# A decoder block on one Trainium2 core: the mixer's output projection as seven block products

## The chip, the cores and the metric

One core of one Trainium2 chip runs the whole kernel, with its five engines: TensorE (PE) for matmuls and transposes, VectorE (DVE), ScalarE (ACT), GpSimd (POOL), and SyncE (SP), which here only issues DMAs. The metric is the device time of one execution in microseconds. Inputs and output are float32 in HBM.

## The reference

One decoder block on 1024 tokens of width 1024. A normed input feeds two branches, a state-space one (S5) and a forgetting attention (FoX). Each is gated, their sum goes through one output projection, and a memory attention and a gated FFN follow:

```python
h = x
u = rms_norm(h, norm_mix)
proj = u @ w_in
...
out_a = glu_a * jax.nn.sigmoid(glu_b)              # glu_a, glu_b = split(gelu(s5) @ w_glu)
out_b = att @ w_fox_o
h = h + (gate_a * out_a + gate_b * out_b) @ w_mix_out
h = h + memory_cross_attention(rms_norm(h, norm_mem_q), rms_norm(mem, norm_mem_kv), w_mem_q, w_mem_kv, w_mem_o)
f_a, f_b = split(rms_norm(h, norm_ffn) @ w_ffn_in)
h = h + (silu(f_a) * f_b) @ w_ffn_out
out = rms_norm(h, norm_final)
```

The line with `w_mix_out`, a product of 1024x1024 by 1024x1024, is the mixer's projection, and the one that is edited.

## The kernel before

**Products.** TensorE works on fp32r operands, which keep fewer bits than fp32. So an operand is split into a high part, a cast on ACT (L183, the helper `split`), and a low part, the rest, by a subtraction on VectorE or GpSimd (L184; GpSimd where `pool_lo` is set). A product is three matmuls, hi·hi, hi·lo and lo·hi, added up in a PSUM bank (`mm3`, L173 to L175). A bank holds 128x512 values. There are eight: three "mm", two "sc", two "pv" and one "misc".

**Order.** The program is written stage by stage, but a scheduler decides the order of each engine's instructions, by priority and by when it expects the operands. Each engine then works through its list in order, and an instruction that waits holds up all behind it. Tiles come from pools with a fixed number of buffers: an allocation waits until the oldest buffer has been read for the last time. `weave(main, side, lead)` mixes two lists of steps in the text; `behind(...)` holds steps back until a named instruction is placed. Nearly all DMAs are issued by SP, in one queue: one that waits holds up the rest.

**The stage of the change** is the first half of `stage_tail`. Activations lie transposed: channels on partitions, tokens along the free axis.

- For each of 8 channel blocks j of 128, `glu.values` and `glu.rest` make the gated unit: products, a copy (L1239), a sigmoid on ACT (L1244), a product on VectorE (L1245) and the gate on GpSimd (L1252) with `ga`, loaded by SP. The result is a tile `sg` of 128x1024.
- `fox_part(j)` (L604) multiplies the attention's output by `w_fox_o` (fox weights, two j at a time), takes the product times the gate half `gb` (L616), adds it to `sg` (L617) and splits the sum into `mT`, the mixer's left operand. It runs three j behind the gated unit.
- `mix_weights` fetches and splits `w_mix_out`. `mix(t, c)` (L664) makes the 128x512 output tile of token tile t and column half c: 8 channel blocks by 3 matmuls, 24, and one VectorE add of the bank to a half-row of x, into H[t] (L668). There are 16 such tiles.
- `ahead(j)` prepares the FFN's weights for j = 0 to 2 (adds and splits on VectorE and ACT, kept in DRAM as `w_d`). Its steps are woven into the first twelve mixer tiles.
- `norm(t)` normalises H[t]: squares on ACT (L190), four small VectorE operations and one GpSimd power (L207 to L217, the power at L211), the scaling of a 128x1024 tile `xs` on VectorE (L231; one buffer), eight transposes in two banks (L237), and splits of the turned blocks into `u2`. Norms 0 to 3 lie behind the last four mixer tiles; norms 4 to 7 are woven with the memory queries `mem_q(h, 0)`, whose weights `wq` are four 128x1024 blocks, split whole.

Of the kernel before, what the change touches and what calls it, by code (L numbers as in the profile page):

```python
# [9 lines left out]
F32 = mybir.dt.float32  # L10
F32R = mybir.dt.float32r
# [3 lines left out]
ALU = mybir.AluOpType  # L15
# [4 lines left out]
P = 128  # L20
D = 1024
L = 1024
NT = 8
# [8 lines left out]
RAW = 1072  # L32

WSLOT = 1088
# [84 lines left out]
class Block:  # L119
# [126 lines left out]
    def norm_turn(self, xs, act, t):  # L246

        for b in range(2):
            cast = self.turned(self.turn(xs, b, ("misc", "pv")[b]), b, act, t)
        return cast  # L250

    def warm(self, n):
# [329 lines left out]
def stage_tail(B, big, s2, sh, x, glu, aT, gate_d, kv_d, w_fox_o, w_mix_out, g_mq, w_mem_q, w_mem_o, g_ffn,  # L582
               w_ffn_in, w_ffn_out, g_fin, out):
    nc, V, A, G, T, S, small, ident = B.nc, B.V, B.A, B.G, B.T, B.S, B.small, B.ident
    NS2 = 16

    def bslot(dt=F32, name="b"):
        return big.tile([P, D], dt, tag="big", name=name)

    def slot(dt=F32, name="t"):  # L590
        return s2.tile([P, D], dt, tag="t", bufs=NS2, name=name)
# [3 lines left out]
    def load(src, name):  # L595
        t_ = sh.half(name)
        S.dma_start(t_, src)
        return t_


    mT = Act(s2, "t", NS2, 8, L, name="mx")
    fox = {}

    def fox_part(j):  # L604
        if j % 2 == 0:
            with B.behind(glu.after):
                fox[j // 2] = B.wblock(w_fox_o, 0, 4, j * P, 2 * P)
        fh, fl = fox[j // 2]
        o = (j % 2) * P
        sg = glu.out.pop(j)  # L610
        for h in range(2):
            cs = slice(512 * h, 512 * h + 512)
            po = B.bank(("pv", "pv", "misc")[(2 * j + h) % 3])
            B.gemm_t(po, fh[:, :, o:o + P], fl[:, :, o:o + P], aT, h, 4)
            gb = load(gate_d[D + j * P:D + (j + 1) * P, cs], "gb")
            V.tensor_mul(gb, gb, po)  # L616
            V.tensor_add(sg[:, cs], sg[:, cs], gb)  # L617
            mh, ml = mT.rhs(j, h)
            merged.append(B.split(mh, ml, sg[:, cs]))

    merged = []
# [8 lines left out]
    for j in range(5, 8):  # L630
        fox_part(j)


    H = [bslot(name=f"h{t}") for t in range(NT)]
    gq = B.bcast_gain(s2, g_mq)
    u2 = Act(s2, "t", NS2, 8, L, name="u2")
# [6 lines left out]
    def wslots(src, pool_lo):  # L643

        nk = src.shape[0] // P
        raw = B.wpool.tile([P, RAW], F32, tag="raw", bufs=4, name="raw")[:, :D]
        S.dma_start(raw.rearrange("p (k c) -> p k c", k=nk), src.rearrange("(k p) c -> p k c", p=P))
        hl = bslot(F32R, "wbh"), bslot(F32R, "wbl")
        B.split(*hl, raw, pool_lo)
        return [t_.rearrange("p (k c) -> p k c", k=nk) for t_ in hl]  # L650

    def mix_weights(c):

        wm = ([], [])
        for kk in range(4):
            if c == 0:
                hl = B.wblock(w_mix_out, 2 * kk, 2, 0, 512)
            else:
                hl = wslots(w_mix_out[2 * kk * P:(2 * kk + 2) * P, 512:D], False)
            for w_, t_ in zip(wm, hl):  # L660
                w_ += [t_[:, 0, :], t_[:, 1, :]]
        return wm

    def mix(t, c, wm):  # L664
        cs = slice(512 * c, 512 * c + 512)
        ps = B.bank()
        gemm_n(ps, mT, t, wm, 8)
        V.tensor_add(H[t][:, cs], ps, load(x[t * P:(t + 1) * P, cs], "xr"))  # L668

    def norm(t, gb, act):  # L670
        xs = s2.tile([P, D], F32, tag="xs", bufs=1, name="xs")
        B.norm_scale(xs, H[t], B.rstd(H[t]), gb)
        return B.norm_turn(xs, act, t)


    AHEAD_IN = 2
# [1 line left out]
    pre = {}  # L678

    def ahead(j):  # L680
# [52 lines left out]

        return [fetch, plain, sums, seventh, rest] if j < AHEAD_IN else [first, plain]

    wm0 = mix_weights(0)
    with B.behind(merged[-1]):
        wm1 = mix_weights(1)
    mixes = [lambda t=t: mix(t, 0, wm0) for t in range(NT)] + [lambda t=t: mix(t, 1, wm1) for t in range(4)]
# [268 lines left out]
    gs = {}  # L1008

    def gated(p):  # L1010
        ge, go = gs.pop(2 * p), gs.pop(2 * p + 1)
# [979 lines left out]
```

## Time and profile before

| what | value |
|---|---|
| median of 3 runs | 1540.18 us (1540.08 to 1541.64) |
| span of the profiled execution | 1538.1 us |
| that execution's own time beside its span | not recorded; the median of the runs is 2.1 us above the span |
| TensorE busy | 1520.7 us (99%) |
| VectorE busy | 1005.7 us (65%) |
| ScalarE busy | 658.1 us (43%) |
| GpSimd busy | 253.6 us (16%) |
| first and last add of the mixer's tiles to H | 692.6 and 769.8 us |

Times in the trace count from the start of the span. A line of a view names the kernel's line, the engine, the operation, the tiles (written<-read), the shape and how often. In a group "| busy, mean ns of one | idle before <-releaser" follow: the busy sum, the mean duration, and how long the engine stood idle just before, with what ended that. In a timeline a row starts with its start and its duration, and square brackets hold the idle time before it. Matmuls overlap, so a matmul's own duration is longer than its distance to the next.

### The profile page before, as it was taken

What the parts mean: (1) busy time and instruction counts of PE and PEld (TensorE: products, weight loads), DVE (VectorE), ACT (ScalarE), POOL (GpSimd) and SP (SyncE); (2) the same over time, 40 slices, a digit from 0 to 9 for tenths busy, and PEclk for the clock granted to TensorE, in tenths of its full rate; (3) what the DMA queues carried; (4) which work ended last, traced back from release to release, by engine and by line L of the source; (5) the groups of instructions that cost most, each with busy time, mean ns of one, the idle gap of its engine ahead of it and who ended that gap; (6) DMA issues with size and microseconds to landing.
All of it is one profiled execution on the core that took longest, in us unless ns stands there. A gap on an engine that the chain in (4) does not pass through costs nothing. (4 is left out here: it accounts for less than half of the span.)

```text
span 1538.1 us, 20434 instructions
## 1 busy us (share of the span) xinstructions
PE 1520.7 (99%) x7329; PEld 1257.7 (82%) x7329; DVE 1005.7 (65%) x1828; ACT 658.1 (43%) x1183; POOL 253.6 (16%) x341
## 2 busy tenths in 40 slices
PE   8999999999999999999999999999999999999998
PEld 7888888898777678888888888888888888888886
DVE  7936554355878867675556797777777775675555
ACT  7423334324667643232435663333333333354343
POOL 1166542100121214100102200000000000101001
PEclk9999999999999999999999999999999999999999
DMA  9634556611223746378210356555544544896542
GB/s 286 161 104 102 131 128 144 180 41 16 50 46 88 192 131 198 111 218 308 89 69 1 117 204 210 162 161 160 158 158 157 157 145 139 291 391 220 192 163 110
DMA packets 196293, 234.06 MB, mean 152 GB/s; under 512 B 35576, under 2 KB 127656, under 8 KB 195680
## 3 DMA queue, kind: packets, MB, share of 16 engines
q1 hardware_dynamic: 188704, 214.93, 47.0%
q10 hardware_dynamic: 7488, 17.83, 3.1%
q8 instruction: 57, 0.93, 0.3%
q14 instruction: 44, 0.36, 0.1%
HBM read 161.94 MB, written 72.71 MB: 153 GB/s over the span
## 5 line engine op out<-in xcount | busy, mean ns | idle before, releaser
L184 DVE TENSOR_TENSOR wlo<-raw,whi 128x1024 fp32r<-128x1024 f32 (+2 forms) x120 | 126.3, 1058 | 45.4 <-ACT whi L183 44.2
L183 ACT CAST whi<-raw 128x1024 fp32r<-128x1024 f32 (+2 forms) x120 | 108.7, 910 | 105.6 <-PE mm L174 39.1
L184 DVE TENSOR_TENSOR ol<-or,oh 128x1024 fp32r<-128x1024 f32 x73 | 90.1, 1236 | 74.0 <-ACT oh L183 71.9
L173 PE MATMUL mm<-uh,whi 128*128 128x512 f32 x344 | 136.5, 397 | 0.0
L174 PE MATMUL mm<-ul,whi 128*128 128x512 f32 x344 | 135.1, 393 | 0.0
L175 PE MATMUL mm<-uh,wlo 128*128 128x512 f32 x344 | 134.5, 391 | 0.0
L183 ACT CAST oh<-or 128x1024 fp32r<-128x1024 f32 x73 | 76.9, 1054 | 105.0 <-PE mm L1108 34.2
L997 POOL TENSOR_TENSOR g<-a,c 128x512 f32<-128x512 f32 x22 | 35.7, 1621 | 389.0 <-ACT a L996 389.0
L175 PEld LDWEIGHTS mm<-uh,wlo 128*128 128x128 f32 x344 | 64.7, 188 | 13.3 <-DVE wlo L184 0.2
L1803 POOL TENSOR_TENSOR pl<-pf,ph 128x512 fp32r<-128x512 f32 (+1 forms) x32 | 36.8, 1152 | 232.5 <-DVE ph L1802 193.3
L173 PEld LDWEIGHTS mm<-uh,whi 128*128 128x128 f32 x344 | 64.8, 188 | 11.6
L174 PEld LDWEIGHTS mm<-ul,whi 128*128 128x128 f32 x344 | 64.8, 188 | 11.0
L1800 ACT ACTIVATE pf<-sc 128x512 f32<-128x512 f32 (+1 forms) x96 | 46.4, 489 | 44.5 <-DVE sc L1796 28.3
L986 DVE SCALAR_TENSOR_TENSOR c<-c,pv 128x512 f32<-128x512 f32 x22 | 15.1, 687 | 76.5 <-ACT c L985 76.4
L211 POOL TENSOR_TENSOR r<-ms,mhalf 128x1 f32<-128x1 f32 (+1 forms) x26 | 15.7, 605 | 298.6 <-DVE ms L207 258.5
L964 PE MATMUL pv<-S3h,we 128*128 128x512 f32 x176 | 57.7, 389 | 0.0
L1806 DVE TENSOR_TENSOR pl<-pf,ph 128x512 fp32r<-128x512 f32 (+2 forms) x64 | 35.3, 553 | 10.4 <-ACT ph L1805 9.8
L1108 PE MATMUL mm<-ol,oh 128*128 128x512 f32 (+1 forms) x110 | 41.9, 381 | 0.0
L1108 PE MATMUL mm<-oh,ol 128*128 128x512 f32 (+1 forms) x110 | 41.9, 381 | 0.0
L1108 PE MATMUL mm<-oh 128*128 128x512 f32 (+1 forms) x110 | 41.9, 381 | 0.0
L173 PE MATMUL sc<-uh,whi 128*128 128x512 f32 x104 | 40.8, 392 | 0.0
L173 PE MATMUL mm<-yh,whi 128*128 128x512 f32 x104 | 40.7, 392 | 0.0
(639 smaller groups left out, 4554.2 us busy)
## 6 DMA issues: line engine op xcount, KB each, us to landing
or<-c_d SPq DMA_DIRECT2D x77, 256.0 KB
wo<-in_w_ffn_out_dram SPq DMA_DIRECT2D x22, 512.0 KB
c_d<-g SPq DMA_DIRECT2D x44, 256.0 KB
t_d<-wo SPq DMA_DIRECT2D x44, 256.0 KB
or<-t_d SPq DMA_DIRECT2D x44, 256.0 KB
rawb<-in_w_ffn_in_dram SPq DMA_DIRECT2D x20, 512.0 KB
raw<-in_w_ffn_in_dram SPq DMA_DIRECT2D x20, 512.0 KB
raw<-in_w_in_dram SPq DMA_DIRECT2D x19, 512.0 KB
```

The lines of the kernel that those rows point to most:

```text
L173: T.matmul(ps, lh, rh, start=first, stop=False)
L174: T.matmul(ps, lh, rl, start=False, stop=False)
L175: return T.matmul(ps, ll, rh, start=False, stop=last)
L183: cast = self.A.copy(hi, src)
L184: self.rest = (self.G if pool_lo else self.V).tensor_sub(lo, src, f32(hi))
L211: self.G.tensor_tensor(out=r, in0=v, in1=self.mhalf[:, 0:n], op=ALU.pow)
L964: T.matmul(ps, l_[:, k, :], r_, start=first and k == 0 and i == 0, stop=k == 3 and i == 2, skip_group_check=True)
L997: G.tensor_mul(g[:, 512:], a1, c1)
L1108: T.matmul(ps, l_[:, gi], r_[:, c0:c1], start=k == 0 and (p == NP - LAST if own else p == 0 and n in (1, 2, 7)), stop=p == NP - 1 and k == ...
L1800: self.exp = A.activation(pf[:, off:], ps[:, off:], AF.Exp)
L1803: G.tensor_sub(pl[:, off:], pf[:, off:], f32(ph[:, off:]))
L1806: self.left = V.tensor_sub(pl[:, off:], pf[:, off:], f32(ph[:, off:]))
```

## The change

The 1024x1024x1024 product is taken as a 2x2 by 2x2 block product (halves of channels and of tokens; halves of channels and of columns) and done by seven block products in place of eight. Each takes a sum or difference of blocks of the activations and of the weights.

- **Activations:** `fox_part` no longer splits the merged rows. It writes them in fp32 to slots m1, m4, m2 (the block A21 stays in `sg`), and `merged_pair` makes m7, m5, m6 and m3 from them with four VectorE operations for each pair of channel blocks. Seven blocks by four channel blocks stay on chip in fp32.
- **Weights:** for each of four pairs of channel blocks, `mix_fetch` loads two whole row blocks of `w_mix_out`, `mix_sums` makes four sums with GpSimd, `mix_store` writes them to DRAM (`mt_d`). The loop over the gated unit's j holds these, at j = 0 to 3, 1 to 4 and 2 to 5.
- **Products:** 28 steps (product n by channel block p, in the order n = 1, 6, 7, 5, 4, 2, 3). `m_get` loads a weight block of 128x512 and splits it (ACT, GpSimd) and the kept activation block (ACT, VectorE), four steps ahead. `m_step` is 12 matmuls into four banks; after p = 3 the banks are added to or subtracted from H in place (`m_add`). x is loaded straight into H. Product 2 goes tile by tile (`m_tile`) over its four channel blocks.
- **Around it:** `ahead` is woven with steps 2 to 19, and its first split is no longer held behind the merge; norms 0 to 3 are woven with the last eight steps and turn through the "pv" banks; the fox parts 5 to 7 stand between the first steps. Norms 4 to 7 and the memory queries are as they were.

```diff
@@ fox_part
-            V.tensor_add(sg[:, cs], sg[:, cs], gb)
-            mh, ml = mT.rhs(j, h)
-            merged.append(B.split(mh, ml, sg[:, cs]))
+            n = ((None, 1), (4, 2))[j % 2][h]
+            dst = block(n, j // 2) if n else sg[:, cs]
+            V.tensor_add(dst, sg[:, cs], gb)
+        if j % 2 == 0:
+            gs[j // 2] = sg[:, :512]
+        else:
+            merged_pair(j // 2)
...
+    def merged_pair(p):
+        a21 = gs.pop(p)
+        a11, a12, s1 = block(1, p), block(2, p), block(5, p)
+        V.tensor_sub(block(7, p), a11, a21)
+        V.tensor_sub(s1, block(4, p), a21)
+        V.scalar_tensor_tensor(out=block(6, p), in0=s1, scalar=-1.0, in1=a11, op0=ALU.mult, op1=ALU.subtract)
+        V.scalar_tensor_tensor(out=block(3, p), in0=block(6, p), scalar=-1.0, in1=a12, op0=ALU.mult, op1=ALU.subtract)
...
+    def mix_sums(p):
+        w1, w2 = msum[p]
+        b11, b12, b21, b22 = w1[:, :512], w1[:, 512:], w2[:, :512], w2[:, 512:]
+        for o, i in ((b11, b12), (b12, b22), (b22, b11), (b21, b22)):
+            G.tensor_add(o, o, i)
...
         glu.rest(j)
+        if j < 4:
+            mix_fetch(j)
+        if 0 < j < 5:
+            mix_sums(j - 1)
+        if 1 < j < 6:
+            mix_store(j - 2)
         if j > 2:
             fox_part(j - 3)
...
+    def m_get(m):
+        n, p = mseq[m]
+        rb = B.wpool.tile([P, RAW], F32, tag="raw", bufs=4, name="raw")[:, :512]
...
+        S.dma_start(rb, src)
+        if m < 4:
+            hl = [B.wpool.tile([P, WSLOT], F32R, tag=t_, name=t_)[:, :D] for t_ in ("whi", "wlo")]
+        else:
+            hl = bslot(F32R, "moh"), bslot(F32R, "mol")
+        B.split(hl[0][:, :512], hl[1][:, :512], mblk[n, p])
+        B.split(hl[0][:, 512:], hl[1][:, 512:], rb, True)
+        mops[m] = hl
...
+    def m_step(m):
...
+        for i in range(4):
+            m_mm(m, i, set_[i])
+        if p == 3:
+            for i in range(4):
+                m_add(n, i, set_[i])
...
-            with B.behind(merged[-1]):
-                B.split(*hl, pre[j][0])
+            B.split(*hl, pre[j][0])
...
-    weave(mixes, [f for j in range(AHEAD_IN + 1) for f in ahead(j)], 4)
-    for t in range(4, NT):
-        mix(t, 1, wm1)
-        norm(t - 4, gq, u2)
+    weave([lambda m=m: m_next(m) for m in range(2, 20)], [f for j in range(AHEAD_IN + 1) for f in ahead(j)], 4)
+    last = [lambda i=i: (m_tile(i), m_next(20 + i)) for i in range(4)] + [lambda m=m: m_step(m) for m in range(24, 28)]
+    weave(last, [lambda t=t: norm(t, gq, u2, ("pv", "pv")) for t in range(4)])
```

What the scheduler makes of it at three places follows. First VectorE near the end of the mixer, before: the stretch from the add of token tile 5 to the normed rows `xs` of norm 3 (an xs reads h0 to h3; `u2l` are splits of turned blocks, `ms` and `rt` small ones of a norm).

```order
L668 TENSOR_TENSOR h5_6798<-sc_7341,xr_7366 128x512
L184 TENSOR_TENSOR u2l0_0_6811<-misc_7382,u2h0_0_6803 128x2x128
L231 SCALAR_TENSOR_TENSOR xs_7428<-h2_6795,r01_7433,gbc_6801 128x1024
L184 TENSOR_TENSOR u2l1_0_6813<-misc_7382,u2h1_0_6805 128x2x128
L184 TENSOR_TENSOR u2l2_0_6815<-pv_7391,u2h2_0_6807 128x2x128
L207 TENSOR_SCALAR ms1_7639<-ss_7636 128x1
L215 TENSOR_TENSOR rt1_7641<-r01_7640 128x1
L184 TENSOR_TENSOR u2l3_0_6817<-pv_7391,u2h3_0_6809 128x2x128
L216 SCALAR_TENSOR_TENSOR rt1_7641<-rt1_7641,ms1_7639 128x1
L217 SCALAR_TENSOR_TENSOR r01_7640<-rt1_7641,r01_7640 128x1
L668 TENSOR_TENSOR h6_6799<-mm_7400,xr_7425 128x512
```

And the same engine in the changed kernel, up to the xs of norm 3 (`wlo` are the splits of the query weights).

```order
L184 TENSOR_TENSOR u2l0_0_6718<-pv_7584,u2h0_0_6710 128x2x128
L184 TENSOR_TENSOR u2l2_0_6722<-pv_7593,u2h2_0_6714 128x2x128
L710 TENSOR_TENSOR h7_6709<-h7_6709,mm_6849 128x512
L184 TENSOR_TENSOR u2l1_0_6720<-pv_7584,u2h1_0_6712 128x2x128
L184 TENSOR_TENSOR u2l3_0_6724<-pv_7593,u2h3_0_6716 128x2x128
L215 TENSOR_TENSOR rt1_7636<-r01_7635 128x1
L184 TENSOR_TENSOR wlo_7684<-raw_7681,whi_7683 128x1024
L216 SCALAR_TENSOR_TENSOR rt1_7636<-rt1_7636,ms1_7634 128x1
L184 TENSOR_TENSOR wlo_7690<-raw_7687,whi_7689 128x1024
L217 SCALAR_TENSOR_TENSOR r01_7635<-rt1_7636,r01_7635 128x1
L207 TENSOR_SCALAR ms1_7724<-ss_7721 128x1
L231 SCALAR_TENSOR_TENSOR xs_7630<-h3_6705,r01_7635,gbc_6932 128x1024
```

Before, one norm stood between two adds, and the query weights' splits 20 rows and more ahead of it; now these splits and the last adds stand between the norms.

TensorE in the changed kernel, at the end of the mixer: the last two tiles of step 27, the transposes of norms 2 and 3, and the first memory query.

```order
L703 MATMUL mm_6848<-moh_7510 128x512
L703 MATMUL mm_6848<-mol_7511,moh_7510 128x512
L703 MATMUL mm_6848<-moh_7510,mol_7511 128x512
L237 MATMUL pv_7584<-ident_69,xs_7571 128x128 x4
L237 MATMUL pv_7593<-ident_69,xs_7571 128x128 x4
L703 MATMUL mm_6849<-moh_7510 128x512
L703 MATMUL mm_6849<-mol_7511,moh_7510 128x512
L703 MATMUL mm_6849<-moh_7510,mol_7511 128x512
L237 MATMUL pv_7643<-ident_69,xs_7630 128x128 x4
L237 MATMUL pv_7652<-ident_69,xs_7630 128x128 x4
L173 MATMUL mm_7693<-u2h0_0_6710,whi_7671 128x512
L174 MATMUL mm_7693<-u2l0_0_6718,whi_7671 128x512
```

Before, the last mixer tile's 24 matmuls stood between the transposes of norm 2 and those of norm 3; now three matmuls do.

SP's queue in the changed kernel, in the gated unit's stage, up to the first gate halves `gb` of the merge (`ws1` and `ws2` are the whole weight rows, `mt_d` the stored sums).

```order
L1337 DMA ga_6122<-gate_d_79 128x512
L1337 DMA ga_6125<-gate_d_79 128x512
L648 DMA ws1_6128<-in_w_mix_out_dram 128x1024
L648 DMA ws2_6129<-in_w_mix_out_dram 128x1024
L659 DMA mt_d_6001<-ws1_6040 128x512 x2
L659 DMA mt_d_6001<-ws2_6041 128x512 x2
L1337 DMA ga_6172<-gate_d_79 128x512
L1337 DMA ga_6175<-gate_d_79 128x512
L648 DMA ws1_6178<-in_w_mix_out_dram 128x1024
L648 DMA ws2_6179<-in_w_mix_out_dram 128x1024
L659 DMA mt_d_6001<-ws1_6082 128x512 x2
L659 DMA mt_d_6001<-ws2_6083 128x512 x2
```

The first two loads of `gb` (gb_6209 and gb_6226) are the next rows; before, they stood behind `ga` loads alone, with no store ahead of them that waits for GpSimd.

More of the change, by code (lines that the diff above doesn't have):

```diff
@@ L598, in load @@
         return t_
-    mT = Act(s2, "t", NS2, 8, L, name="mx")
-    fox = {}
+    fox, gs, done = {}, {}, {}
+    mt_d = B.dram.tile([8, 4, P, 512], F32, name="mt_d")
+    mblk = {}
     def fox_part(j):
@@ L635, in stage_tail, with m_x @@
+    def m_x(t):
+        S.dma_start(H[t], x[t * P:(t + 1) * P, :])
+    MAHEAD = 4
+    for t in range(4, NT):
+        m_x(t)
+    fox_part(5)
+    for m in range(3):
+        m_get(m)
+    fox_part(6)
+    m_get(3)
+    m_step(0)
+    m_step(1)
+    for t in range(4):
+        m_x(t)
+    fox_part(7)
+    m_get(4)
+    m_get(5)
     gq = B.bcast_gain(s2, g_mq)
-    u2 = Act(s2, "t", NS2, 8, L, name="u2")
     def gemm_n(ps, act, t, w, nk):
@@ L641, in gemm_n, with norm @@
             B.mm3(ps, ah, al, w[0][k], w[1][k], k == 0, k == nk - 1)
[L643 to L670, printed above, removed]
+    def norm(t, gb, act, banks=("misc", "pv")):
         xs = s2.tile([P, D], F32, tag="xs", bufs=1, name="xs")
         B.norm_scale(xs, H[t], B.rstd(H[t]), gb)
-        return B.norm_turn(xs, act, t)
+        return B.norm_turn(xs, act, t, banks)
     AHEAD_IN = 2
@@ L1007, in stage_tail @@
     t_d = B.dram.tile([8, NP, P, 512], F32, name="t_d")
-    gs = {}
     def gated(p):
```

63 lines of the change are left out of this document (54 added, 9 removed).

## The prediction

> **What bounds the kernel now.** I first read the page's head and its chain of waits, to see which engine sets the end.
>
> ```profile
> span 1538.1 us, 20434 instructions
> PE 1520.7 (99%) x7329; PEld 1257.7 (82%) x7329; DVE 1005.7 (65%) x1828; ACT 658.1 (43%) x1183; POOL 253.6 (16%) x341
> PE 45%; DVE 1%; issue 0%; ACT 0%; POOL 0%; POOLq 0%; ACTq 0%; DVEq 0%
> ```
>
> TensorE is busy for 99% of the span, and what the chain attributes is nearly all TensorE. An average over stages says little about one stage, so next come windows over the stage that is edited: gated unit and merge (580 to 680 us), the mixer's projection (683 to 770), the memory queries behind it. The columns after each window are its length and then the busy time of PE, PEld, DVE, ACT and POOL, the granted clock, the DMA share and GB/s.
>
> ```profile
> 580.00:600.00 20.00, 20.00 (x90) 16.55 (x89) 15.82 (x11) 6.57 (x9) 11.18 (x6) 1.00 0.77 232
> 660.00:680.00 20.00, 20.00 (x90) 16.57 (x89) 16.02 (x24) 5.48 (x9) 3.00 (x2) 1.00 0.64 197
> 720.00:740.00 20.00, 20.00 (x90) 16.57 (x89) 10.84 (x15) 7.92 (x13) 0.56 (x1) 1.00 0.91 328
> 760.00:780.00 20.00, 19.97 (x100) 16.47 (x100) 11.03 (x30) 6.46 (x19) 1.65 (x3) 1.00 0.00 1
> 780.00:800.00 20.00, 19.92 (x101) 16.54 (x100) 9.47 (x20) 7.67 (x18) 0.00 (x0) 1.00 0.31 117
> ```
>
> TensorE has no gap here, at a granted clock of 1.00, so there is nothing to win by a wait that goes. A gain can only be matmuls that are not issued, and every gap that the change opens on TensorE is a loss. VectorE has 4 to 10 us free in each window of 20.
>
> The last piece of the method is the timeline of TensorE where mixer and memory queries meet.
>
> ```profile
> 766.16 0.39 PE L173 MATMUL mm<-wbh,mxh 128*128 128x512 f32 x1
> ...
> 769.33 0.40 PE L175 MATMUL mm<-wbh,mxl 128*128 128x512 f32 x1
> 769.57 0.60 PE L237 MATMUL misc<-ident,xs 128*128 128x128 f32 x4
> 770.00 0.60 PE L237 MATMUL pv<-ident,xs 128*128 128x128 f32 x4
> 770.63 0.50 PE L173 MATMUL sc<-u2h,whi 128*128 128x512 f32 x1
> ```
>
> The first two rows are 14 matmuls apart (766.16 to 769.33), 0.226 us each; a duration of 0.39 is longer because matmuls overlap. Eight transposes take 769.57 to 770.63, 1.06 us, 0.13 each. The seam between the stages is closed.
>
> **Part 1: matmuls that go.** Before, the mixer is 16 tiles of 24 matmuls, 384; now it is 28 steps of 12, 336. 48 × 0.226 = **−10.9 us**, if TensorE stays fed. The other parts are what feeding it costs.
>
> **Part 2: sums and stores in the gated unit's stage.** Sixteen GpSimd adds and sixteen stores go in among GpSimd's gates and SP's loads. Rows, in order: the gates as a group, GpSimd and SP at the point in question, and VectorE waiting for the first gate_b half.
>
> ```profile
> L1252 POOL TENSOR_TENSOR sg<-sg,ga 128x512 f32<-128x512 f32 x15 | 23.9, 1610 | 57.1 <-DVE sg L1245 49.8 <-DMA ga<-gate_d 7.3
> 600.13 2.53 POOL L1252 TENSOR_TENSOR sg<-sg,ga 128x512 f32<-128x512 f32 x2 [0.42 <-DMA ga<-gate_d]
> 598.13 1.92 SPq L597 DMA_DIRECT2D gb<-gate_d  x2
> 601.94 0.69 DVE L616 TENSOR_TENSOR gb<-gb,pv 128x512 f32<-128x512 f32 x1 [3.23 <-DMA gb<-gate_d]
> 592.77 0.39 PE L173 MATMUL pv<-ath,whi 128*128 128x512 f32 x1
> ```
>
> An add of this form takes 2.53 / 2 = 1.27 us undisturbed and 1.61 on average: 16 are 20 to 26 us, and GpSimd is idle for 57 us in front of this group, so as work they hide. The path goes through SP's queue: the first gate_b load stands behind eight stores, and the last of these wait for the eighth sum. The sums of two fetches (10 to 13 us) and three pairs of gates (7.6 to 9.7) end at 608 to 613 us if they start near 590; the load then takes what it took before, 598.13 to 601.94, 3.8 us. VectorE's product with it, which frees a pv bank, comes at 612 to 616 instead of 601.94. TensorE, which starts the merge's products at 592.77 in the last row, has 90 matmuls ahead of the first that needs that bank (the merge's first two products, the gated unit's four for j = 4, a third, and half of one for j = 5): until 613. VectorE also holds gates and splits behind that load, in its order. No row shows this wait; its ends are 0 and 6 us, and I take **+3**.
>
> **Part 3: merges and the first steps.** The four block merges of a pair cost VectorE 4 × 0.69 but replace sixteen splits, so nothing here. What is left are the last two parts of the merge, where the weights of the first steps share slots with the fox weights, and GpSimd runs the weight blocks' subtractions. I take **+1** (0 to 3), from the slack of VectorE in the window 660 to 680 (16.02 of 20).
>
> **Part 4: the steady steps.** Twelve matmuls are 2.72 us. Over 17 steps, 46.2 us, VectorE has one 128x512 subtraction and on average one H add in each (17 × 2 × 0.60, the pitch of part 5), and the FFN's precomputation, which was there before: ten adds and ten subtractions of 512 and three of 1024 columns (20 × 0.60 + 3 × 1.14). That is 35.8 us, 10.4 free. GpSimd gets one subtraction in a step, 1.27. I take **+0.3** for the phase of the four banks between two products. Two rows below speak for more, and are rivals.
>
> **Part 5: the seam.** Before, norms 0 to 3 lay in the mixer's last four tiles, one in 5.4 us of matmuls, and the query weights' splits before them. Now the norms, the last six H adds, four weight-block splits and the four query-weight splits lie in VectorE's order between the add of tile 6 (rows 4 to 7 of the output) and the normed rows xs of norm 3. Durations are from these rows:
>
> ```profile
> L231 DVE SCALAR_TENSOR_TENSOR xs<-h,r,gbc 128x1024 f32<-128x1024 f32 x5 | 6.4, 1277 | 0.0
> L184 DVE TENSOR_TENSOR wlo<-raw,whi 128x1024 fp32r<-128x1024 f32 x15 | 18.3, 1220 | 7.0 <-ACT whi L183 6.9
> L668 DVE TENSOR_TENSOR h<-mm,xr 128x512 f32<-128x512 f32 x10 | 6.9, 688 | 6.3 <-PE mm L175 6.3
> L184 DVE TENSOR_TENSOR u2l<-misc,u2h 128x256 fp32r<-128x256 f32 x8 | 3.4, 420 | 0.6
> L215 DVE TENSOR_TENSOR rt<-r 128x1 f32<-128x1 f32 x8 | 1.3, 160 | 5.3 <-POOL r L211 5.3
> 733.80 0.69 DVE L668 TENSOR_TENSOR h<-sc,xr 128x512 f32<-128x512 f32 x1
> 734.40 1.22 DVE L184 TENSOR_TENSOR wlo<-raw,whi 128x1024 fp32r<-128x1024 f32 x1
> 735.53 0.21 DVE L207 TENSOR_SCALAR ms<-ss 128x1 f32<-128x1 f32 x1
> 736.41 0.16 DVE L215 TENSOR_TENSOR rt<-r 128x1 f32<-128x1 f32 x1 [0.67 <-POOL r L211]
> 736.61 0.16 DVE L216 SCALAR_TENSOR_TENSOR rt<-rt,ms 128x1 f32<-128x1 f32 x1
> ```
>
> Queued instructions overlap by some 0.08 us (733.80 to 734.40 is 0.60 for a duration of 0.69), so I use 0.60, 1.14, 1.20, 0.34 and 0.20 for the small ones. The stretch holds 4 xs (4.8), 4 query-weight splits (4.6), 6 adds and 4 block splits of 512 (6.0), 12 u2 splits (4.1) and 15 small ones (3.0): 22.5 us. TensorE has in the same stretch 60 matmuls (13.6) and 24 transposes (3.2): 16.8 us. It runs dry for 5.7. Then it turns norm 3 (1.06) while VectorE goes through 12 small instructions (2.4) and the first u2 split (0.34): less the first product, another 1.5. That makes 7.2 with no wait on VectorE. Waits add to it: two of the GpSimd powers stand right before their reader (0.67 each), four GpSimd subtractions overlap VectorE (up to 0.65 each, below), and the last H adds wait for matmuls that were themselves held up. I take **+12**, with 7 and 14 as ends. The cover that is gone is plain: behind the last mixer matmul TensorE's order has nothing but the transposes of norm 3 and the products that need it.
>
> Norms 4 to 7 lie between memory queries as before, and of the parts behind them nothing is moved: 0.
>
> **The sum** against the profiled execution: −10.9 + 3 + 1 + 0.3 + 12 = +5.4. That execution's span is 1538.1; its own time with what lies around the span isn't given, and the median of three, 1540.18, is 2.1 above it. I add the change to the median: 1545.6, say **1545.5 us**.
>
> [...] GpSimd and VectorE disturb each other here:
>
> ```profile
> 614.73 0.69 DVE L616 TENSOR_TENSOR gb<-gb,pv 128x512 f32<-128x512 f32 x1 [0.17 <-PE pv L175]
> 629.36 1.34 DVE L617 TENSOR_TENSOR sg<-sg,gb 128x512 f32<-128x512 f32 x1
> 628.86 3.00 POOL L1252 TENSOR_TENSOR sg<-sg,ga 128x512 f32<-128x512 f32 x2 [13.14 <-DVE sg L1245]
> L617 DVE TENSOR_TENSOR sg<-sg,gb 128x512 f32<-128x512 f32 x16 | 13.5, 844 | 0.2
> ```
>
> An add of two SBUF tiles takes 1.34 inside a GpSimd pair, 0.65 more than the 0.69 it takes alone, and the pair takes 3.00 for 2.53; a VectorE product with a PSUM operand keeps its 0.69 inside such a pair. [...]
>
> [...]
>
> **Rivals.**
>
> *The seam holds, and it is faster.* VectorE's stretch could start ahead: if the squares and sums of norms 0 and 1 are done while product 2's tiles run, and the GpSimd and H-add waits overlap TensorE's own, the seam costs its 5.7 + 1.5, and sums and stores hide. For it: TensorE's 20.00 of 20.00 with the same kinds of instructions before. Against it: VectorE's 22.5 us are a sum of fixed work. It decides where part 5 and part 2 together fall under 10.7. Then −10.9 + 7.2 + 0 to 1 is −3.7 to −2.7, about 1537; with half of the 7.2 hidden as well, 1533.
>
> [...] A step leaves VectorE 0.6 us (10.4 over 17). If each of the 17 GpSimd subtractions stretches a VectorE split by 0.65, 11 us is added against the 10.4 free, and the H adds and the blocks for TensorE come late: +3 to +6, 1549 to 1552. For it: the rows above. Against it: blocks are made four steps (10.9 us) ahead.
>
> *A transfer at the head of a queue.* The precomputation's ACT and VectorE instructions wait for DMAs:
>
> ```profile
> L183 ACT CAST wph<-wpr 128x1024 fp32r<-128x1024 f32 x3 | 3.1, 1049 | 12.3 <-DMA wpr<-in_w_ffn_in_dram 12.3
> L184 DVE TENSOR_TENSOR wpl<-wpr,wph 128x512 fp32r<-128x512 f32 x8 | 5.4, 685 | 7.9 <-DMA w_d<-wph 7.9
> ```
>
> Before, nothing urgent was queued behind them. Now the splits of the next steps' blocks are. Four steps of lead hide one wait of 7.9; two in a row, or 12.3 at once, leave TensorE waiting for 2 to 4 us: 1548 to 1550.
>
> *It doesn't save matmuls' time.* If the steps' matmuls took longer than 0.226 us, since each step changes banks at every third matmul, part 1 would shrink. The fox and mixer matmuls run at one pitch in all banks (20.00 of 20.00), so I give this next to nothing.
>
> **Chances.** My forecast, the seam at 7 to 14 and the sums at 0 to 6 with the rest covered: 0.55; all lower ends together give 1536.3, all upper ones 1552.6. Faster with the seam at its floor or less: 0.25. The lock: 0.1. The transfers: 0.1. A measurement of this kernel can tell 0.2%, 3.1 us, from no change. All of the two last and about two thirds of the first lie above 1543.3: slower 0.55. Within 3.1 us: 0.2. Faster than 1537.1: 0.25. The range that holds 8 in 10 leaves out a tenth on each side: 1533 to 1553. The likeliest case's own range is 1541 to 1550.
>
> **What would show it.** In the profile after: TensorE's groups of the mixer with 336 matmuls and the rest unchanged; in the windows, TensorE at 20.00 through the steady steps, and some 12 us less than its length over the 30 us from product 2's tiles to the second memory query, with VectorE near full; in the waits, transposes of xs waiting for VectorE L231. In the gated unit's stage, one wait of some 3 us at a pv bank, its releaser VectorE's product with gb, and that one's the DMA gb. Wrong would be: a seam of under 5 us, gaps in the steps between (a wait on moh, mol or H adds), or a gated stage that waits more than 6.

## The result: slower by 1.4%

The changed kernel takes 1562.68 us (1561.93 to 1563.58, 4 runs), the kernel before 1540.66 (4 runs): a ratio of 1.0143, 95% interval 1.0129 to 1.0157. The forecast was 1545.5 us, with a range up to 1553.

The profile after, first the head of its page:

```profile
span 1561.9 us, 20543 instructions
PE 1521.4 (97%) x7281; PEld 1254.9 (80%) x7281; DVE 1044.7 (67%) x1860; ACT 670.2 (43%) x1215; POOL 319.8 (20%) x385
```

TensorE has 48 instructions fewer (7281 for 7329), yet its busy time did not fall: what 48 matmuls saved, slower matmuls took back. Next the windows that answer to those of before (length, busy PE, PEld, DVE, ACT, POOL, granted clock, DMA share, GB/s):

```profile
600.00:620.00 20.00, 13.19 (x59) 10.58 (x57) 6.73 (x5) 2.25 (x3) 19.53 (x15) 0.93 0.70 252
640.00:660.00 20.00, 20.00 (x90) 16.57 (x89) 14.11 (x16) 3.37 (x6) 7.92 (x6) 1.00 0.51 157
660.00:680.00 20.00, 20.00 (x90) 16.44 (x89) 14.53 (x17) 3.39 (x5) 4.65 (x4) 1.00 0.87 285
700.00:720.00 20.00, 17.25 (x64) 13.70 (x63) 17.95 (x25) 6.85 (x12) 6.61 (x4) 0.83 0.43 142
780.00:800.00 20.00, 13.79 (x63) 11.14 (x62) 13.83 (x38) 9.43 (x27) 3.14 (x4) 0.83 0.26 80
```

The granted clock, 1.00 in every window shown of before, is 0.83 to 0.93 wherever TensorE isn't busy throughout; from 640 to 680, where it is, the clock is 1.00 as before. The gaps, as the waits of TensorE between 560 and 840 us (total, times, longest):

```profile
PE pv L237 <- DVE xs L231: 8.8, 2, 5.9
PE pv L173 <- DVE gb L617: 7.9, 1, 7.9
PE mm L703 <- DVE h L710: 3.0, 1, 3.0
PE sc L703 <- DVE h L710: 2.8, 1, 2.8
PE mm L174 <- DVE u2l L184: 0.3, 1, 0.3
```

Together 22.8 us. The earliest of them, on TensorE's timeline (start, duration, and in brackets the wait ahead), shows what comes behind a wait:

```profile
612.80 0.39 PE L175 MATMUL mm<-yh,wlo 128*128 128x512 f32 x1
621.05 0.79 PE L173 MATMUL pv<-ath,whi 128*128 128x512 f32 x1 [7.86 <-DVE gb L617]
621.64 0.63 PE L174 MATMUL pv<-atl,whi 128*128 128x512 f32 x1
622.07 0.63 PE L175 MATMUL pv<-ath,wlo 128*128 128x512 f32 x1
...
624.13 0.39 PE L174 MATMUL pv<-atl,whi 128*128 128x512 f32 x1
```

The same stretch in windows of 2 us, for the granted clock (the third number from the end):

```profile
618.00:620.00 2.00, 0.00 (x0) 0.00 (x0) 1.01 (x1) 0.60 (x1) 2.00 (x3) 0.50 0.00 0
622.00:624.00 2.00, 2.00 (x6) 1.54 (x5) 1.88 (x2) 0.00 (x0) 1.92 (x2) 0.50 0.99 375
624.00:626.00 2.00, 2.00 (x10) 1.65 (x10) 0.00 (x0) 0.00 (x0) 1.92 (x2) 0.99 0.81 281
```

Behind the wait the pitch is 0.43 us (621.64 to 622.07) in place of 0.23, until about 3 us after the restart; the clock fell to 0.50 while TensorE waited. Added up over the timeline, the slow matmuls and transposes behind the five long waits cost 1.6, 2.9, 1.7, 1.5 and 2.4 us more than at full pitch: 10.1 us. (Of the last 2.4, 1.2 lie behind the wait of 0.3 us, which falls into the slow stretch behind norm 3.) The whole loss can be read without adding up single matmuls, from the first product of the merge to the first memory scores, before and after (TensorE alone: length, busy time, granted clock, DMA share, GB/s):

```profile
592.77:796.77 204.00, 203.90 (x930) 1.00 0.50 165
592.63:819.44 226.81, 203.97 (x883) 0.94 0.61 200
```

TensorE is busy as long as before, with 48 matmuls fewer (47 by these counts, which take in the windows' edges). So matmuls and transposes that ran slower took back the 10.9 us: 11.0 in all. Then −10.9 + 22.8 + 11.0 = +22.9 us. The first memory scores start 22.7 us later than before, and the spans differ by 23.8; about 1 us lies behind this stretch.

### The profile page after: what moved, and what is told of

Same layout as the page of the kernel before. It is cut to its first block, busy times and chain, and to the rows that moved or that the text cites. A ratio compares the mean times of both kernels' runs of the same rounds, so it can differ in the third digit from the quotient of the medians.

```text
span 1561.9 us, 20543 instructions
## 1 busy us (share of the span) xinstructions
PE 1521.4 (97%) x7281; PEld 1254.9 (80%) x7281; DVE 1044.7 (67%) x1860; ACT 670.2 (43%) x1215; POOL 319.8 (20%) x385
## 4 chain that ended last, share of the span: by engine, by line
PE 86%; DVE 7%; ACT 2%; issue 2%; POOL 2%; DMA 2%; SPq 0%; POOLq 0%; ACTq 0%; DVEq 0%
PE mm L1051 15%; PE pv L1051 8%; PE mm L173 8%; PE mm L175 8%; PE mm L174 8%; PE mm L1194 5%; PE sc L1051 4%; PE sc L1194 4%; PE sc L173 3%; PE sc L175 3%; PE sc L174 3%; PE pv L1194 3%; PE misc L1194 2%; PE mm L703 1%; PE sc L1879 1%
## 5 line engine op out<-in xcount | busy, mean ns | idle before, releaser
L184 DVE TENSOR_TENSOR wlo<-raw,whi 128x1024 fp32r<-128x1024 f32 (+2 forms) x116 | 122.1, 1058 | 40.6 <-ACT whi L183 39.4
L173 PEld LDWEIGHTS mm<-uh,whi 128*128 128x128 f32 x344 | 64.8, 188 | 11.5
L184 POOL TENSOR_TENSOR mol<-raw,moh 128x512 fp32r<-128x512 f32 x24 | 37.8, 1586 | 44.2 <-ACT moh L183 25.4
L1072 ACT COPY c<-mm 128x512 f32<-128x512 f32 x22 | 12.9, 587 | 65.1 <-PE mm L1051 65.1
```

The source lines that it names most:

```text
L173: T.matmul(ps, lh, rh, start=first, stop=False)
L184: self.rest = (self.G if pool_lo else self.V).tensor_sub(lo, src, f32(hi))
```

## The experiments

After the trace my theory had four parts: the sums hold up GpSimd and SP in the gated unit's stage; VectorE has too much to do in the steps; its list sets the seam; and each wait costs more than its length, by the clock. Each edit is made to the changed kernel, 1.0143, but for stall and stall_warm, whose base is the kernel before; each ratio below is to runs of the kernel before on the same chip.

**Who holds the first gate product, GpSimd or SP?** The timelines of GpSimd, ACT and VectorE in the changed kernel give this chain: the gate of j = 3 on GpSimd, a sigmoid on ACT, VectorE, the product with gb.

```profile
615.85 1.26 POOL L654 TENSOR_TENSOR ws<-ws 128x512 f32<-128x512 f32 x1
617.06 2.48 POOL L1338 TENSOR_TENSOR sg<-sg,ga 128x512 f32<-128x512 f32 x2
618.36 0.60 ACT L1330 ACTIVATE sb<-sc 128x512 f32<-128x512 f32 x1 [7.51 <-POOL sg L1338]
618.99 1.49 DVE L1331 TENSOR_TENSOR sg<-sg,sb 128x512 f32<-128x512 f32 x1 [5.55 <-ACT sb L1330]
620.32 1.27 DVE L617 TENSOR_TENSOR gb<-gb,pv 128x512 f32<-128x512 f32 x2
```

GpSimd had its sums ahead of the gate, the sigmoid needed the half-tile that the gate reads, and the product with gb stood behind the gated rows in VectorE's order. The load of gb was issued at 609.40, long before. Two runs:

```diff
-        if 0 < j < 5:
-            mix_sums(j - 1)
-        if 1 < j < 6:
-            mix_store(j - 2)
+        if 2 < j < 7:                      # sums_late
+            with B.behind(glu.gated):
+                mix_sums(j - 3)
+        if j > 3:
+            mix_store(j - 4)
```
```diff
-        if 1 < j < 6:
-            mix_store(j - 2)
+        if j > 3:                          # stores_late
+            mix_store(j - 4)
```

> The weight sums of pair p are held behind the gate of j = 3 + p on GpSimd, and their stores come behind the first gate_b loads in SP's queue; everything else as in the changed kernel (1562.7 us). Theory A (GpSimd's order: the gate of j = 3 stands behind twelve sums, and the half-tile it holds delays a sigmoid, VectorE and a PSUM bank): TensorE's wait of 7.9 us at 613 us falls under 1.5, and with it the half-clock stretch of some 1.5 us behind it: 1553 to 1555 us. Theory B (SP's queue: the first gate_b load stands behind eight stores that wait for sums): the same here, so this run alone does not part the two; the next one does. Theory C (neither; the wait is of DMA bandwidth): the wait stays at 6 or more, 1561 to 1563 us.

> Only the stores of the weight sums move: in SP's queue they now stand behind the first gate_b loads. The sums stay where they were in GpSimd's order, eleven of them ahead of the gate of j = 3 (twelve before). Theory A (GpSimd's order): TensorE still waits 6 to 8 us at the pv bank near 613 us, 1560 to 1563 us. Theory B (SP's queue, as the prediction had it): the wait falls under 1.5, 1553 to 1555 us.

Measured: sums_late 1.0192 (1.0177 to 1.0207), 1569.13 us; stores_late 1.0167 (1.0150 to 1.0184), 1564.46 us. Neither gained, and sums_late lost some 7 us more, so theory A failed as I had put it, and theory B with it: in both runs the wait at the pv bank went, and another came some 10 us later, of 5.6 us in sums_late (with one more of 3.4 at 677) and of 8.4 in stores_late. In stores_late TensorE waits for VectorE's copy of a gated product. Ahead of that copy, VectorE waited 5.7 us for a gb load; and SP, before it issued that load at 622.78, had waited 8.6 us for a gate on GpSimd, which had to read its ga tile before the next ga load could overwrite it. The rows of VectorE, SP and ACT in this stage of stores_late:

```profile
626.55 0.69 DVE L617 TENSOR_TENSOR gb<-gb,misc 128x512 f32<-128x512 f32 x1 [5.71 <-DMA gb<-gate_d]
SPq L1337 <- POOL sg L1338: 8.6, 1, 8.6
ACT sb L1330 <- POOL sg L1338: 20.7, 2, 15.0
```

SP and ACT both wait for gates, and the gates stand behind sums on GpSimd. It was not one queue or the other; whatever is queued behind a sum that isn't done waits.

**What do the sums cost as a whole?** The fetches, sums and stores are left out; steps 4 to 27 read plain weight blocks in place of the sums, so the output is another.

```diff
-        if j < 4:
-            mix_fetch(j)
-        if 0 < j < 5:
-            mix_sums(j - 1)
-        if 1 < j < 6:
-            mix_store(j - 2)
...
-            src = mt_d[n, p]
+            src = w_mix_out[j * P:(j + 1) * P, c:c + 512]
```

> The weight rows' fetches, the sixteen GpSimd sums and the sixteen stores are left out, and steps 4 to 27 read plain blocks of the weight matrix (the mixer's result isn't the reference's); all matmuls, splits and adds stay. This prices part 2 whole. Theory (sums that end late hold up what stands behind them on GpSimd and behind their stores on SP): TensorE has no wait between 600 and 690 us, and the time is 7.9 us plus 1.5 to 2.5 us of half clock shorter than the changed kernel's 1562.7: 1552 to 1554 us. Rival (the first gate products are late for another reason, DMA bandwidth or the fox weights): a wait of 3 us or more stays there, 1557 us or more.

Measured: 1.0084 (1.0069 to 1.0099), 1553.48 us, and no wait of TensorE between 580 and 690. So part 2 cost some 9 us, as the theory had it: 7.9 of waiting and 1.6 of slow matmuls behind it.

**Can the sums be hidden where they are?** Two orders that take gates and loads out of their way. sums_spread holds the sums of pair p behind the gate of j = 3 + p and writes all stores behind the loop in the text (the scheduler still queued the first of them at 609 us); hold_stores also holds each pair's stores behind the gb loads two parts on.

```diff
+        if 2 < j < 7:
+            with B.behind(glu.gated):
+                mix_sums(j - 3)
...
+        if j > 4:                          # hold_stores; sums_spread stores behind the loop
+            with B.behind(loaded[0]):
+                mix_store(j - 5)
```

> The sums of pair p are held behind the gate of j = 3 + p on GpSimd, and all stores are written behind the loop over j, so that the gated unit's and fox weights' loads for the next parts are ahead of them on SP. Nothing is left out. Theory (the waits of the two earlier versions came from one cause, sums that end near 626 us with loads and gates queued behind them): no wait over 1.5 us between 600 and 690 us, 1553 to 1556 us, as without sums. Rival (the sums' GpSimd time can't be hidden in this stage at all): a wait of 4 us or more remains at some other place, 1560 us or more.

> Sums held as in sums_spread, and in SP's queue the stores of pair p are held behind the gate_b loads of part p + 2, when their sums are long done; so neither a gate on GpSimd nor a load on SP stands behind a sum that isn't done. Nothing is left out. Theory (in sums_spread the stores still blocked SP for 5.4 us at a time, and that was the whole rest): no wait over 1.5 us between 600 and 690 us, 1552 to 1556 us, as with the sums left out. Rival (the sums cost this stage by their stretching of VectorE, wherever they stand): a wait of 3 us or more remains, 1557 us or more.

Measured: sums_spread 1.0170 (1.0153 to 1.0187), 1566.82 us, with waits of 7.1 and 3.5 us in this stage. hold_stores 1.0140 (1.0125 to 1.0155), 1562.76 us, with 2.6 and 3.0. In both the theory missed, and the time and the wait that was left are those of the rival. In the changed kernel SP waited at the stores for GpSimd's sums, 8.7 us in seven waits between 580 and 640 us: the first two sets of four stores took 5.09 and 4.46 us there, and the last, behind the last sum, 2.10. The timeline of SP's queue in sums_spread shows such a long set again:

```profile
608.99 5.41 SPq L659 DMA_DIRECT2D mt_d<-ws  x4
614.45 0.92 SPq L1338 DMA_DIRECT2D ga<-gate_d  x2
```

Four stores take 5.41 us there, with the loads of ga behind them. In hold_stores the first two sets of four take 2.1 each; the other two take 5.0 and 3.0, for a reason that no row shows. But the stores were not the whole rest: the waits became shorter and more, each with its slow matmuls (pitch 0.43 us). I found no order in this stage in which the sums were free. Whether the sums' stretching of VectorE is what remains, as the rival has it, is not shown.

**Is it GpSimd's help or its disturbance?** The weight blocks' low parts go from GpSimd to VectorE.

```diff
-        B.split(hl[0][:, 512:], hl[1][:, 512:], rb, True)
+        B.split(hl[0][:, 512:], hl[1][:, 512:], rb)
```

> The low parts of the 28 weight blocks are made on VectorE in place of GpSimd; nothing else is changed. Lock theory (each GpSimd subtraction stretches VectorE's two-SBUF-operand instructions by as much as the subtraction would cost VectorE itself): VectorE gets 28 x 0.60 = 17 us more instructions and loses some 17 us of stretching, its busy time from 680 to 800 us stays at 99 us within 4, its subtractions are at 0.69 us again in place of 1.04, and the time is the same within 4 us: 1559 to 1566 us. Load theory (GpSimd relieves VectorE): VectorE, busy for 83% of that stretch already, gets 17 us more, and the waits of the H adds and of the seam grow by 6 to 12 us with their clock loss: 1570 us or more.

Measured: 1.0150 (1.0135 to 1.0165), 1562.73 us: the same. The stretch from 680 to 800 us as one window (columns as above), first of the changed kernel, then of no_pool_split:

```profile
680.00:800.00 120.00, 105.10 (x444) 85.14 (x443) 99.14 (x152) 56.98 (x117) 44.95 (x33) 0.91 0.58 189
```

```profile
680.00:800.00 120.00, 104.54 (x448) 84.06 (x447) 95.47 (x178) 57.17 (x119) 6.31 (x8) 0.91 0.56 190
```

And VectorE's groups there (count | busy time, mean ns of one | idle time ahead), of the changed kernel and of no_pool_split:

```profile
L184 DVE TENSOR_TENSOR mol<-m,moh 128x512 fp32r<-128x512 f32 x24 | 25.0, 1043 | 5.5 <-ACT moh L183 5.5
L710 DVE TENSOR_TENSOR h<-h,mm 128x512 f32<-128x512 f32 x12 | 7.9, 680 | 2.8 <-PE mm L703 2.8
```

```profile
L184 DVE TENSOR_TENSOR mol<-m,moh 128x512 fp32r<-128x512 f32 x24 | 16.5, 686 | 2.2 <-ACT moh L183 2.2
L184 DVE TENSOR_TENSOR mol<-raw,moh 128x512 fp32r<-128x512 f32 x24 | 16.4, 685 | 0.5 <-ACT moh L183 0.5
```

VectorE does 24 subtractions more in that stretch, 16.4 us, and is busy for 3.7 us less. So GpSimd's instructions there had stretched VectorE's by about 20 us: mol from 0.69 to 1.04, while an H add, which reads PSUM, stays at 0.68. TensorE's waits in no_pool_split add up to much the same, with 7.4 us for H adds, 7.2 in the gated unit's stage and 7.9 at the seam. Having the subtractions on GpSimd relieved nothing.

**Are the H adds late because VectorE is full?** The arithmetic of the FFN's precomputation is left out of the steps; its transfers stay, and store what was loaded, so the output is another.

```diff
-        return [fetch, plain, sums, seventh, rest] if j < AHEAD_IN else [first, plain]
+        def stores(a, b):
+            for n in range(a, b):
+                keep(n, pre[j][0])
+
+        return [fetch] + [lambda a=a: stores(a, a + 2) for a in (0, 2, 4)] + [lambda: stores(6, 7)] if j < AHEAD_IN \
+            else [first, lambda: stores(0, 2)]
```

> The precomputation of the FFN's weights for j = 0 to 2 keeps its loads and stores but makes nothing: its casts, adds and subtractions on ACT and VectorE (about 19 us of VectorE at unstretched durations) are left out, and the FFN reads raw weights there (the output isn't the reference's). Theory (in the steps VectorE has too much to do, its own work and GpSimd's stretching together): both waits for H adds (2.8 and 3.0 us) go, with 3 to 5 us of half clock: 1551 to 1556 us; the waits at 613 us and at the seam stay within 1.5 us of what they were. Rival (the H adds are late because four banks are added in a row, whatever else VectorE does): the two waits stay at 2 us or more, 1560 us or more.

Measured: 1.0108 (1.0093 to 1.0123), 1557.16 us. The waits for H adds fall from 2.8 and 3.0 to one of 2.2; the second is a wait of 0.7 for GpSimd. The wait at 613 stays (8.0). A new one of 5.9 us comes at 677 to 683, for a gb load (VectorE's own wait for it is 11.5 us), which the run wasn't meant to make. At the seam the two waits for xs, 8.8 us, became one of 2.7, which the expectation had not foreseen either: the precomputation's arithmetic may weigh on the seam too, but the new wait ahead of it leaves that open. So the second wait goes with VectorE's load, with the same reserve; of the first, most remains (2.3 remain in combo2 below, too, where the first split of the precomputation stands behind these adds). There VectorE still has the last merges, stretched by GpSimd, ahead of the H adds; no run takes the merges away, so that they make this wait is argued and not shown. VectorE's timeline in the changed kernel:

```profile
695.53 1.77 DVE L184 TENSOR_TENSOR mol<-m,moh 128x512 fp32r<-128x512 f32 x1
697.23 1.78 DVE L639 TENSOR_TENSOR m<-m,sg 128x512 f32<-128x512 f32 x1
...
700.73 1.21 DVE L184 TENSOR_TENSOR wpl<-wpr,wph 128x1024 fp32r<-128x1024 f32 x1
701.86 0.68 DVE L641 SCALAR_TENSOR_TENSOR m<-m,m 128x512 f32<-128x512 f32 x1
702.46 1.27 DVE L710 TENSOR_TENSOR h<-h,sc 128x512 f32<-128x512 f32 x2
```

**Does VectorE's list set the seam?**

```diff
-    wq = [B.wblock(w_mem_q, 0, 8, h * P, P) for h in range(MH)]
+    wq = [B.wblock(w_mem_q, 0, 8, 0, P)]
+    with B.behind(*ends[-1]):              # norm 3's last cast and last subtraction
+        wq += [B.wblock(w_mem_q, 0, 8, h * P, P) for h in range(1, MH)]
```

> The splits of the query weights 1 to 3 are held behind norm 3's splits on ACT and VectorE; the first stays. Three subtractions of 1.14 us and three casts of 1.05 us leave the stretch before norm 3's normed rows. Theory (VectorE's list sets the seam): the two waits for xs, 8.8 us together, fall to 3 to 5, one half-clock stretch goes or shrinks, and the time is 4 to 8 us below the changed kernel: 1555 to 1559 us. Rival (the norm's own chain of squares, GpSimd's power and small operations sets the seam): the waits stay at 8 or more, 1561 to 1563 us.

Measured: 1.0094 (1.0079 to 1.0109), 1555.13 us, 7.5 us below the changed kernel. TensorE's waits from 690 us on:

```profile
PE pv L237 <- DVE xs L231: 2.9, 1, 2.9
PE sc L703 <- DVE h L710: 2.8, 1, 2.8
PE mm L703 <- DVE h L710: 2.6, 1, 2.6
PE mm L174 <- DVE u2l L184: 0.7, 1, 0.7
```

The wait of 5.9 us for norm 3 is gone, its slow matmuls with it. The spans of the two profiled executions differ by 9.8 us; some 7.5 of these lie at the seam, and 1.9 at 613, where the wait is 6.0 in place of 7.9 though the edit doesn't touch that stage. Three splits that nobody needed yet had stood in front of the rows that TensorE waited for. This was the cheapest repair of all.

**The clock.** warm_seam puts 50 small matmuls where TensorE waits for norm 3. stall and stall_warm start from the kernel before: three waits made on purpose, without and with 45 small matmuls ahead of each of the four norms.

```diff
+            if t == 3:
+                B.warm(50)                 # warm_seam, ahead of norm 3
...
+        for _ in range(8 if act is u2 and t < 4 else 1):    # stall, stall_warm
+            B.norm_scale(xs, H[t], r, gb)
+        if act is u2 and t < 4:                             # stall_warm
+            B.warm(45)
...
+        with B.behind(B.turning if t > 4 else None):        # stall, stall_warm
+            mix(t, 1, wm1)
```

> Fifty extra small bf16 matmuls on constant data (some 0.107 us each at full clock, 5.4 in all) are put into TensorE's order ahead of norm 3's transposes, where it waits 5.9 us for the normed rows; they add work that computes nothing. Clock theory (TensorE's granted clock falls to half after some 2 to 4 us without matmuls and comes back only after some 3 to 6 us of work): the transposes and matmuls behind them run at full pitch, 0.23 us in place of 0.43, and the time falls by 2 to 3 us: 1559.5 to 1561 us. Rival (the slow matmuls behind a wait are slow for another reason, such as operands that come late): the pitch behind them stays at 0.43, and the time stays at 1562.7 us or rises by the part of the extra matmuls that stands in the way, up to 1 us.

> The kernel before, with waits made on purpose: in norms 0 to 3 the scaling to xs on VectorE is done eight times over (same values, some 8.4 us more for each norm), and each of the last three mixer tiles is held on TensorE behind the transposes of the norm ahead of it, so that TensorE waits three or four times for about 5 us, with nothing else in the kernel changed. Clock theory: each wait costs its length and 1.5 to 3 us more, in matmuls at 0.43 us in place of 0.23; with 15 to 20 us of waits the time is 1540 + 15 to 20 + 6 to 10 = 1561 to 1570 us, 6 to 10 us more than the waits in the trace account for. Rival (a wait costs its length, no more): the time is 1540 plus the waits in the trace, within 2 us.

> As stall, with 45 small bf16 matmuls on constant data (some 5 us) in TensorE's order ahead of each of the four norms' transposes, where it would wait. Clock theory: the granted clock stays at 1.00 in these stretches, no matmul runs at 0.43, and the time is 5 to 10 us below stall's. Rival (the slow matmuls come from late operands or from VectorE's and the banks' contention): the time is stall's, within 2 us, or up to 2 us above where the small matmuls overrun a wait.

Measured: warm_seam 1.0137 (1.0122 to 1.0152), 1560.89 us: not to be told from the base by its time. In its trace the fifty small matmuls take 5.63 us, 0.11 each, the transposes of norm 3 take 1.06 us in place of 1.94, and the matmuls behind them run at 0.23. stall 1.0170 (1.0155 to 1.0185), 1566.67 us; stall_warm 1.0163 (1.0146 to 1.0180), 1565.14 us, so the 5 to 10 us between them didn't come. The traces tell why. A window over the norms, of stall and then of stall_warm, the clock again third from the end:

```profile
765.00:775.00 10.00, 8.51 (x31) 7.19 (x32) 8.17 (x13) 1.39 (x4) 0.55 (x1) 0.67 0.00 0
```

```profile
765.00:775.00 10.00, 8.20 (x50) 6.65 (x48) 9.19 (x13) 1.49 (x4) 0.55 (x1) 1.00 0.01 2
```

And TensorE's timeline there, the first transposes of two norms with the waits ahead of them, of stall and of stall_warm:

```profile
766.50 1.08 PE L237 MATMUL misc<-ident,xs 128*128 128x128 f32 x4 [8.61 <-DVE xs L231]
781.49 1.09 PE L237 MATMUL misc<-ident,xs 128*128 128x128 f32 x4 [6.03 <-DVE xs L231]
```

```profile
749.54 5.09 PE L258 MATMUL sc<-ident 128*128 128x256 bf16 x45
767.73 0.63 PE L237 MATMUL misc<-ident,xs 128*128 128x128 f32 x4 [1.80 <-DVE xs L231]
781.02 0.63 PE L237 MATMUL misc<-ident,xs 128*128 128x128 f32 x4 [1.82 <-DVE xs L231]
```

With the small matmuls the clock stays at 1.00, and a cycle from one norm's transposes to the next takes 13.29 us (767.73 to 781.02) in place of 14.99 and, the next one, 14.4: 1.1 to 1.7 us per wait are the clock's. But the first block of 45, at 749.54, stood where TensorE had no wait, and cost its 5.09 us. stall itself is 26.7 us above the kernel before for waits of 20.7 us in all: 2.0 us more per wait. So much is shown: half clock behind a wait cost 1.5 to 2.9 us beyond the wait's length in the changed kernel and 2.0 on average in stall, and the small matmuls in stall's waits saved 1.1 to 1.7 of it.

How long after a stop the clock falls, the trace of the changed kernel shows for its five waits of 2.8 us and more: the granted clock went to 0.50 between 2.0 and 4.0 us after TensorE ran out of work (at the wait of 3.0 us that was 0.8 us behind the restart), and it was back at 1.00 between 2.8 and 6.1 us after the restart. Over the runs there was half clock during and behind waits of 5.6 to 8.6 us, with full pitch again some 3 to 5 us after the restart, over 6 in a few. The shorter waits differ among themselves: of the 31 waits of 2.2 to 3.1 us in the changed kernel and the runs made from it, 23 were followed by half clock, which cost 1.4 to 2.9 us, and eight lost 0.5 us or less (behind a wait of 2.75, 2.9 us in the changed kernel and 0.1 or less in stores_late).

**All repairs together.** combo2 is hold_stores and wq_lazy, with the first split of the precomputation held behind the H adds of product 1 and its last three pieces moved behind norm 3.

```diff
-    weave([lambda m=m: m_next(m) for m in range(2, 20)], [f for j in range(AHEAD_IN + 1) for f in ahead(j)], 4)
+    pieces = [f for j in range(AHEAD_IN + 1) for f in ahead(j)]
+    weave([lambda m=m: m_next(m) for m in range(2, 20)], pieces[:9], 4)
...
-            B.split(*hl, pre[j][0])
+            with B.behind(added.get(1) if j == 0 else None):
+                B.split(*hl, pre[j][0])
...
+        for f in pieces[9:]:
+            f()
```

> hold_stores and wq_lazy together; the first split of the FFN's precomputation is held behind the H adds of product 1, and its last three pieces move behind norm 3. Nothing is left out. Theory (four separate causes: sums, H adds behind the precomputation on VectorE, the seam's list, and half clock after each wait): 9 us from the sums, 7 from the query weights, 3 to 6 from the H adds come off 1562.7: 1540 to 1546 us, TensorE waiting under 6 us in all from 600 to 800. It beats the kernel before (1540) only if the waits left are under some 4 us with 3 us of half clock. Rival (VectorE's total work from 690 to 800, about 99 us of instructions for 92 us of matmuls, sets the length whatever the order): 1548 us or more.

Measured: 1.0091 (1.0074 to 1.0108), 1554.08 us: the time is in the rival's range, and only 1 us below wq_lazy alone. TensorE's longest waits between 560 and 840 us in combo2:

```profile
PE misc L173 <- DVE gb L619: 3.7, 1, 3.7
PE pv L237 <- DVE u2l L184: 3.1, 1, 3.1
PE mm L173 <- DVE sg L1340: 2.9, 1, 2.9
PE sc L707 <- DVE h L714: 2.3, 1, 2.3
PE misc L237 <- DVE u2l L184: 1.6, 1, 1.6
```

Each wait that was attacked shrank, and others stand in its place, five of 1.6 to 3.7 us, all for VectorE, the three longest with slow matmuls behind them (pitch 0.43 us). VectorE is busy for 89 of the 100 us from 700 to 800. The rival's reason, VectorE's work behind 690, covers that stretch only: the waits of 2.9 and 3.7 lie at 626 and 675 us. No version found here beats the kernel before; whether one exists is open.

## Why the prediction was wrong

The sign and the seam were right; the sum was too small by 18 us against the spans. Most of that is one step, the last below. Two of the prediction's own signs of being wrong came: a gated stage that waits more than 6 us, and waits for H adds.

- **Part 1** (−10.9) held: 48 matmuls fewer, and the pitch was 0.227 wherever TensorE hadn't waited.
- **Part 2** (+3, ends 0 and 6): 7.9 us, above the upper end. The step that failed is "The path goes through SP's queue". That queue did what I had said: it issued the load of gb at 609.40, forecast 608 to 613, and TensorE ran until 613. But VectorE's product came at 620.32 and not at 612 to 616: I followed one queue, and the later release came from GpSimd's gate of j = 3 through ACT and the gated rows ahead in VectorE's list.
- **Part 3** (+1): 0; TensorE is at 20.00 of 20.00 from 640 to 680.
- **Part 4** (+0.3): 5.8, the size of the rival in which GpSimd's subtractions stretch VectorE's splits ("The lock" among the chances, 0.1). The failed step is "35.8 us, 10.4 free", a sum that leaves GpSimd's stretching out. GpSimd's subtractions cost VectorE 20 us for 24, 0.83 each; for the 17 steps that would be 14 us, an estimate, more than the 10.4. I had the 0.65 from one row and held the lead of four steps to cover it. In the worst place it is 1.77 for 0.69, 1.08 us more, nearly a whole GpSimd subtraction (1.28 at the least). No run leaves the subtractions out altogether, so that this stretching makes the waits is argued. And the first of the two, 2.8 us, stands right behind the last merges: it can as well be put to part 3, inside that part's 0 to 3.
- **Part 5** (+12, ends 7 and 14): 8.8 + 0.3 = 9.1. The mechanism and its place were right, as wq_lazy shows.
- **Missing altogether**: 11.0 us of slow matmuls, the largest miss. The step that failed is "The other parts are what feeding it costs": it counted every wait by its length, at full clock behind it. The profile of before could not show the price, since TensorE never waited there in that stretch.

With the measured waits alone the sum would have been +11.9; with the clock, +22.9.

## What to carry to other kernels

Where TensorE is at 100%, look behind each wait for slow matmuls before you count it at its length: the changed kernel's five waits of 2.8 to 7.9 us cost 1.5 to 2.9 us more than that. And prefer a change that opens one long gap to one that opens five: behind one wait of 2.8 us here as much was lost, 2.9 us, as behind one of 8.6, 2.3. Trading TensorE's work for element-wise work needs slack on the engine that takes it, in that very stretch and after contention: GpSimd's subtractions of two SBUF tiles were no relief for VectorE here (with 24 of them on VectorE itself, 16.4 us, it was busy for 3.7 us less). And where instructions are queued early because they could run early, ask what stands behind them: the query weights' splits cost 7.5 us by standing a few rows too soon.

## What the runs showed of the hardware that I had not expected

A GpSimd subtraction of two SBUF tiles, 1.28 us at the least and 1.59 on average, took 0.83 us of VectorE's time where both engines were busy (the prediction had 0.65), and VectorE does the same subtraction itself in 0.69. Of the 31 waits of TensorE of 2.2 to 3.1 us, 23 had half clock behind them. And in the changed kernel four DMA stores whose sums weren't done took 5.1 us of SP's queue, with loads behind them, against 2.1 where the sums were done.
